# A hybrid decoder layer on one core: 1/rms of x and h sent through DRAM to all partitions and read with a stride, a new head, idle matmuls ahead of the last spread

## The chip, the core and the metric

The kernel runs on one core of a Trainium2 chip. The metric is the device time of one execution in microseconds; the medians below are those of repeated executions. The profile is that of one further execution, taken by the hardware profiler. Engines: PE is TensorE (PEld its loading of weights, beside the matmuls), DVE VectorE, ACT ScalarE, POOL GpSimd, SP SyncE. SP does no arithmetic and issues most of the DMAs.

## The reference, cut to what matters

One layer: an HGRN2 group of four heads and a sliding-window attention group of eight heads, both reading the same normed x; an output projection; a gated MLP with a causal depthwise convolution of three taps; a last norm. x is 1 x 2048 x 1024 in float32, the MLP is 2816 wide.

```python
def rmsnorm(x, w, eps=EPS):
    xf = x.astype(jnp.float32)
    inv = lax.rsqrt(jnp.mean(xf * xf, axis=-1, keepdims=True) + eps)
    return (xf * inv * w.astype(jnp.float32)).astype(x.dtype)
...
        u = rmsnorm(h, norm_mix_w[l])
        proj = u @ w_in[l]
...
        mix = jnp.concatenate([o_hg, o_att], axis=-1)
        h = h + mix @ w_out[l]
        v = rmsnorm(h, norm_ffn_w[l])
        gate = causal_depthwise_conv(v @ w_gate[l], conv_w[l], conv_b[l])
        h = h + (jax.nn.silu(gate) * (v @ w_up[l])) @ w_down[l]
    return rmsnorm(h, final_norm_w)
```

The factor 1/rms belongs to a token. Activations lie with features on the 128 partitions and tokens along the row, so the factor must lie, for all 1024 tokens of a half, on every partition. Since it is the same for all features of a token, it is multiplied in after a projection instead of before.

## The kernel before, in words

**Data.** The 2048 tokens go in two halves of 1024 (`HALF`; `hf` counts them). A tile of activations is 128 features by 1024 tokens; D = 1024 makes 8 of them (`KT`). A matmul takes a 128x128 tile of weights and 512 tokens, so that the two blocks of 512 of a half (`halves()`) fill two PSUM banks. Float32 is made of two parts, hi (rounded) and lo (the rest), by ScalarE (hi) and VectorE (lo): `prep` for weights, `split` for activations. Each product is three matmuls: hi·hi, hi·lo, lo·hi.

**Stages of a half.** A *unit* (L194 to L213) is a projection of 128 columns: 8 tiles of x, 48 matmuls. First come the units k and v of attention (`kv`), then f of the first HGRN head (`f0`), and then heads of HGRN and of attention in turn (hq, g, q units, chunk states, scores). Then the output projection with the residual (h), then gate and up: 22 tiles of 128 of the MLP's width, two at a time (`pr` = 0 to 10, a *pair*), first the gate's pair unit, then the up's. A pair unit (L784) is one Strassen-Winograd step: seven products of four tiles each, named by their weights A11, A12, S2, S1, S3, S4, A22, on the banks X, Y, Z, with sums of the banks' copies (s, u) made by ScalarE (copy, L807) and VectorE (add, L904 and L862 to L866). Then the down projection, with the second half's first units beside it, and the last norm.

**1/rms.** `Stats` (L230 to L276) adds the squares of the tiles (square on ScalarE, sum on VectorE) into one tile `acc` (named invb). `inverse` (L249) sums over the partitions with 8 small matmuls against a column of ones (L258, `pst`, 128 tokens each: token c·128+p comes to partition p, column c), takes 1/sqrt on VectorE in some eleven small steps (L160 to L172, without a table), and multiplies the result with the identity into `acc` (L263): a block per 128 tokens with the factors on its diagonal. `spread` (L267) multiplies that with a 128x128 of ones (L273, `pinv`, two matmuls of 512 columns), which sums each column and so puts it on all partitions, and ScalarE copies it back to `acc` (L276).

This is done for x (named "x"), for h after the output projection ("h") and for the last norm ("o", in quarters of a half). Those who multiply with invb: k and v (L336), q of attention (L358), f (L448), q and g of HGRN (L453, L475), the gate's products (L866) and the product behind Silu (L898). `rs`, the [128, 8] tile itself, is used for v of HGRN.

**Order.** Each engine has its own order of instructions. It is written by the order of calls and a scheduler at build, and pinned in places by `tc.issue_after`. The hooks `then` of a unit or pair unit call something ahead of its i-th tile or of a named product. Ahead: x of the first half is loaded and split, k and v are made from x tile by tile, `constants()` follows (its DMAs on ScalarE's queue), then `xs.inverse`, and `xs.spread` in the middle of unit f. In the second half `inverse` stands behind the last tile but one of unit k and `spread` in the middle of unit v. For h, `inverse` is called ahead of product S4 and `spread` ahead of A22 of the first gate unit; the gate's four products with invb wait until then (`later`, `flush`).

**The end.** The last quarter's `inverse` uses ScalarE's Sqrt, then a spread of 256 columns (L273), eight products (L1105) and the output's DMAs.

Of the kernel before, what the change touches and what calls it, by code (L numbers as in the profile page):

```python
# [8 lines left out]
F32 = mybir.dt.float32  # L9
# [8 lines left out]
P = 128  # L18
# [26 lines left out]
WARM = 12  # L45
LV = 4
# [3 lines left out]
def hymba_layer(ctx: ExitStack, tc: tile.TileContext, a: dict, out: bass.AP):  # L50
# [33 lines left out]
    nc.scalar.activation(warm, ones[:, 0:1], AF.Sigmoid)  # L84
# [5 lines left out]
    idle = ps("at", "idle")  # L90
    for _ in range(WARM):
        nc.tensor.matmul(idle[:, 0:P], ones, ones, start=True, stop=True)
# [12 lines left out]
    def constants():  # L105
# [21 lines left out]
        nc.scalar.dma_start(battn, a["b_attn"])  # L127
# [3 lines left out]
        nc.scalar.dma_start(C.hgw, a["hg_norm_w"])  # L131
        C.sinkb = cp.tile([P, ATT_J, 2], F32, name="sinkb")
        nc.scalar.dma_start(C.sinkb.rearrange("p j k -> p (j k)"), a["sinks"].to_broadcast([P, 8]))
        C.nfw = cp.tile([P, KT], F32, name="nfw")
        nc.scalar.dma_start(C.nfw, a["norm_ffn_w"])
        C.fnw = cp.tile([P, KT], F32, name="fnw")
        nc.scalar.dma_start(C.fnw, a["final_norm_w"])
        C.cw = cp.tile([P, FT, 4], F32, name="cw")
        nc.scalar.dma_start(C.cw, a["conv"])

        lbl = cp.tile([P, 2, HG], F32, name="lbl")
        nc.scalar.dma_start(lbl, a["lb_logits"])
# [38 lines left out]
    def prep(src, slots=False, parts=(slice(0, D),), between=[]):  # L181

        raw = raw4(None)
        hi, lo = [hp.tile([P, D], F32R, tag="m", name=f"w{t}", bufs=KT) if slots else
                  wp.tile([P, D], F32R, tag=t, name=f"w{t}", bufs=2) for t in ("hi", "lo")]
        for c in parts:
            nc.sync.dma_start(raw[:, c], src[:, c])
            nc.scalar.copy(hi[:, c], raw[:, c])  # L188
            nc.vector.tensor_tensor(lo[:, c], raw[:, c], hi[:, c].bitcast(F32), op=ALU.subtract)  # L189
            if between:  # L190
                between.pop(0)()
        return hi, lo

    def unit(src, X, name, order=range(KT), kind="mm", then={}, behind={}, in_turn=False):  # L194
# [5 lines left out]
        for both in [[h] for h in halves()] if in_turn else [halves()]:  # L200
            for i, kt in enumerate(order):
# [6 lines left out]
                with tc.issue_after(mark) if mark else ExitStack():  # L208
                    for w, x, f, l in ((wh, xh, kt == order[0], False), (wh, xl, False, False),
                                       (wl, xh, False, kt == order[-1])):  # L210
                        for b, bs in both:
                            nc.tensor.matmul(o[b], w, x[:, bs], start=f, stop=l)  # L212
# [16 lines left out]

    class Stats:  # L230


        def __init__(self, acc, sq=None, eng=None, k=0):
            self.acc, self.sq, self.eng, self.k = acc, sq, eng or [nc.vector], k

        def halves(self):
            n = self.acc.shape[-1] // 2
            return [Stats(self.acc[:, i * n:(i + 1) * n], self.sq, self.eng, self.k) for i in range(2)]

        def add(self, src, apart=False):  # L240
            t = self.acc if self.k == 0 else self.sq()[:, 0:src.shape[-1]] if self.sq else src
            nc.scalar.activation(t, src, AF.Square)
            self.k += 1
            if self.k > 1 and apart:
                return t
            if self.k > 1:
                return self.eng[(self.k - 1) % len(self.eng)].tensor_tensor(self.acc, self.acc, t, op=ALU.add)

        def inverse(self, keep, last=None):  # L249
# [5 lines left out]
            for src in (self.acc, last):  # L255
                if src is not None:
                    for c in range(nt):
                        nc.tensor.matmul(st[:, c:c + 1], src[:, c * P:(c + 1) * P], ones[:, 0:1],  # L258
                                         start=src is self.acc and (c == 0 or last is None), stop=last is None or src is last,
                                         skip_group_check=last is not None)  # L260
            rs = self.rs = rsqrt(st[:, 0:nt], nt, 1.0 / D, keep, last is not None)
            dg = self.acc
# [4 lines left out]
        def spread(self, bank=None):  # L267
# [3 lines left out]
            for b in range(n // w):  # L271
                pb = ps(aux[b % 2 if bank is None else bank], "pinv")[:, 0:w]
                nc.tensor.matmul(pb, ones, self.acc[:, b * w:(b + 1) * w], start=True, stop=True)  # L273
# [11 lines left out]
    def load(hf, X, stage, W=None):  # L285

        st = Stats(inv_tile())
        xt = []

        def part(kt, c):  # L290
            nc.sync.dma_start(xt[kt][:, c], a["xT"][kt, :, hf * HALF + c.start:hf * HALF + c.stop])
            split(xt[kt][:, c], nmw[:, kt:kt + 1], dst=[t[:, c] for t in X[kt]])

        for kt in range(KT):
# [927 lines left out]
```

## Time and profile before

| what | value |
|---|---|
| median of 3 runs | 2199.68 us (2198.82 to 2201.12) |
| profiled execution | 2200.38 us |
| its span, first to last instruction | 2198.7 us, 29491 instructions |
| mean granted clock of TensorE | 0.997 |
| PE busy | 2177.5 us (99%), 11410 matmuls |
| PEld busy | 1831.0 us (83%) |
| DVE busy | 1639.2 us (75%), 2449 instructions |
| ACT busy | 1049.8 us (48%), 1846 instructions |
| POOL busy | 6.4 us, 28 instructions |
| SP's queue (hardware) | 251.70 MB, 33.9% of 16 engines' span |
| ScalarE's queue | 4.34 MB |

The profiled execution lasted 1.7 us longer than its span; it is 0.7 us above the median of the runs. How rows are read: in a timeline row stand start and duration in us, engine, line, operation, output<-inputs, shape, and a count; where several instructions are drawn together, the duration runs from the first one's start to the last one's end; in square brackets stand the idle time of the engine before it and what ended it. In a row of groups stand, behind the bar, busy time, mean ns of one, and idle time before with its releaser. In a row of waits stand the waiting and the releasing instruction and, behind the colon, us in all, how many times, and the longest. In a row of stretches stand length, the busy time of PE, PEld, DVE, ACT and POOL with instructions, the granted clock, the DMA engines' busy share and GB/s. In a row of DMA issues stand count, size of one and the median time from issue to landing.

### The profile page before, as it was taken

The numbers are of one execution on the slowest core, as the hardware profiler recorded it, in microseconds if no ns is written. First come the engines' busy times: TensorE is split into PE (matmuls) and PEld (weight loads), VectorE is DVE, ScalarE is ACT, GpSimd is POOL, SyncE is SP. The second block draws the span as 40 slices with busy tenths as digits, with TensorE's granted clock in tenths as the row PEclk, the third lists the DMA queues.
The fourth block names the chain that finished last, engine by engine and source line by source line (L and its number), as shares of the span: only waits on it lengthen the run. The fifth ranks groups of instructions, "written<-read, shape, count | busy, mean of one in ns | idle before, by whom it ended". The sixth has DMA issues, their size and how long they took to land.

```text
span 2198.7 us, 29491 instructions
## 1 busy us (share of the span) xinstructions
PE 2177.5 (99%) x11410; PEld 1831.0 (83%) x11410; DVE 1639.2 (75%) x2449; ACT 1049.8 (48%) x1846; POOL 6.4 (0%) x28
## 2 busy tenths in 40 slices
PE   9999999999999999999999999999999999999998
PEld 7988988888888888888889889888888888888887
DVE  6568559688887888885855666677888878887766
ACT  5446445454444444435635455535644444443353
POOL 1000000000000000000000000000000000000000
PEclk9999999999999999999999999999999999999999
DMA  4101112322323234974631111114132323259643
GB/s 154 51 30 51 37 35 76 116 77 92 115 94 122 86 123 139 373 251 138 218 133 41 44 36 51 61 36 134 58 127 90 125 92 114 94 185 395 227 144 130
DMA packets 94214, 257.91 MB, mean 117 GB/s; under 512 B 11578, under 2 KB 17402, under 8 KB 94074
## 3 DMA queue, kind: packets, MB, share of 16 engines
q1 hardware_dynamic: 88128, 251.70, 33.9%
q10 hardware_dynamic: 5946, 4.34, 0.7%
q8 instruction: 89, 1.46, 0.3%
q14 instruction: 51, 0.42, 0.1%
HBM read 195.10 MB, written 57.15 MB: 115 GB/s over the span
## 4 chain that ended last, share of the span: by engine, by line
PE 96%; DVE 2%; ACT 0%; DMA 0%; issue 0%; ACTq 0%; DVEq 0%
PE X L800 7%; PE X L801 7%; PE X L802 7%; PE pop L212 7%; PE hq L212 4%; PE q L212 4%; PE f L212 4%; PE g L212 4%; PE pdx L1011 4%; PE Y L802 4%; PE pdx L1013 4%; PE pdx L1012 4%; PE Y L801 4%; PE Y L800 4%; PE pdy L1011 3%; PE pdy L1013 3%
## 5 line engine op out<-in xcount | busy, mean ns | idle before, releaser
L629 ACT CAST whi<-raw 128x1024 fp32r<-128x1024 f32 x88 | 92.7, 1053 | 109.6 <-PE X L801 67.6
L800 PE MATMUL X<-T,whi 128*128 128x512 f32 x352 | 136.9, 389 | 0.0
L801 PE MATMUL X<-T,whi 128*128 128x512 f32 x352 | 136.9, 389 | 0.0
L802 PE MATMUL X<-T,wlo 128*128 128x512 f32 x352 | 136.9, 389 | 0.0
L895 DVE SCALAR_TENSOR_TENSOR y<-ga,cw,y 128x1024 f32<-128x1024 f32 x88 | 112.3, 1278 | 26.0 <-ACT y L893 25.9
L807 ACT COPY u<-X 128x512 f32<-128x512 f32 x88 | 51.4, 584 | 134.2 <-PE X L802 134.1
L188 ACT CAST whi<-raw 128x1024 fp32r<-128x1024 f32 (+2 forms) x61 | 62.8, 1034 | 96.9 <-PE q L212 31.9
L630 DVE TENSOR_TENSOR wlo<-raw,whi 128x1024 fp32r<-128x1024 f32 x88 | 107.1, 1217 | 0.0
L630 DVE TENSOR_TENSOR xld<-raw,xhd 128x1024 fp32r<-128x1024 f32 x72 | 80.7, 1131 | 19.2 <-ACT xhd L629 18.8
L629 ACT CAST xhd<-raw 128x1024 fp32r<-128x1024 f32 x72 | 69.7, 978 | 41.6 <-DMA raw<-act0T 13.6
L212 PE MATMUL pop<-XL,whi 128*128 128x512 f32 x256 | 85.9, 393 | 2.1 <-DVE XL L224 2.1
L212 PE MATMUL pop<-XH,wlo 128*128 128x512 f32 x256 | 85.0, 391 | 0.8 <-DVE wlo L189 0.8
L212 PE MATMUL pop<-XH,whi 128*128 128x512 f32 x256 | 84.8, 396 | 0.2
L189 DVE TENSOR_TENSOR wlo<-raw,whi 128x1024 fp32r<-128x1024 f32 (+2 forms) x61 | 73.2, 1204 | 10.5 <-ACT whi L188 10.5
L801 PEld LDWEIGHTS X<-T,whi 128*128 128x128 f32 x352 | 66.1, 188 | 13.8
L802 PEld LDWEIGHTS X<-T,wlo 128*128 128x128 f32 x352 | 66.1, 188 | 13.7
L800 PEld LDWEIGHTS X<-T,whi 128*128 128x128 f32 x352 | 66.0, 188 | 13.7
L1011 PE MATMUL pdx<-xhd,hid 128*128 128x512 f32 x192 | 74.5, 392 | 1.0 <-ACT hid L629 1.0
L1012 PE MATMUL pdx<-xld,hid 128*128 128x512 f32 x192 | 74.7, 389 | 0.0
L1013 PE MATMUL pdx<-xhd,lod 128*128 128x512 f32 x192 | 73.7, 389 | 0.0
L621 PE MATMUL pvv<-whi,XH 128*128 128x256 f32 x256 | 73.5, 288 | 0.0
L622 PE MATMUL pvv<-whi,XL 128*128 128x256 f32 x256 | 72.6, 284 | 0.0
(368 smaller groups left out, 6547.0 us busy)
## 6 DMA issues: line engine op xcount, KB each, us to landing
wr<-in_w_down SPq DMA_DIRECT2D x90, 512.0 KB, 4.8
raw<-in_w_gate SPq DMA_DIRECT2D x44, 512.0 KB, 3.6
raw<-in_w_up SPq DMA_DIRECT2D x44, 512.0 KB, 3.7
raw<-act0T SPq DMA_DIRECT2D x20, 512.0 KB, 5.7
raw<-act1T SPq DMA_DIRECT2D x20, 512.0 KB, 10.1
act0B<-y SPq DMA_DIRECT2D x33, 256.0 KB, 2.6
act1B<-y SPq DMA_DIRECT2D x33, 256.0 KB, 2.5
raw<-in_w_out SPq DMA_DIRECT2D x16, 512.0 KB, 4.6
```

Source lines behind the costliest of these rows:

```text
L189: nc.vector.tensor_tensor(lo[:, c], raw[:, c], hi[:, c].bitcast(F32), op=ALU.subtract)
L212: nc.tensor.matmul(o[b], w, x[:, bs], start=f, stop=l)
L621: nc.tensor.matmul(o[:, 0:256], xh[:, t], hi[:, c], start=kt == 0, stop=False)
L629: return (nc.scalar.copy(h, src), (eng or nc.vector).tensor_tensor(l, src, h.bitcast(F32), op=ALU.subtract))
L630: (eng or nc.vector).tensor_tensor(l, src, h.bitcast(F32), op=ALU.subtract))
L800: nc.tensor.matmul(o, wh[:, ws], xh, start=i == 0 and not more, stop=False, skip_group_check=more)
L801: nc.tensor.matmul(o, wh[:, ws], xl, start=False, stop=False, skip_group_check=more)
L802: r = nc.tensor.matmul(o, wl[:, ws], xh, start=False, stop=i == 3, skip_group_check=more)
L895: nc.vector.scalar_tensor_tensor(y, g[:, w:w + HALF], C.cw[:, ft, w:w + 1], y, op0=ALU.mult, op1=ALU.add)
L1011: nc.tensor.matmul(o, wh[:, i, c], ah[:, i, cols], start=f, stop=False, skip_group_check=more)
L1012: nc.tensor.matmul(o, wh[:, i, c], al[:, i, cols], start=False, stop=False, skip_group_check=more)
L1013: nc.tensor.matmul(o, wl[:, i, c], ah[:, i, cols], start=False, stop=l, skip_group_check=more)
```

## The change

1. **x and h.** With `sent=True`, `inverse` ends behind 1/sqrt: GpSimd's queue writes the [128, 8] tile to DRAM as it lies (`row`, 4 KB), and a second DMA of the same queue reads these 1024 numbers to all 128 partitions of `acc` (512 KB). As it lies means partition by partition: the number of token c·128+p stands at p·8+c. So `every()` gives a reader a view with steps of 8 elements (32 bytes) for neighbouring tokens, and the readers' other operands go through `by_tile()`. The product with the identity, the spread's two matmuls and the two copies are gone for x and h of both halves; they stay for the last norm.
2. **The head.** `head()` replaces `load` and `first_unit` for the first half. The first k weights come in three parts over SP's and ScalarE's queues, steps of k and v alternate, squares of x come where `turn` puts them, the constants' DMAs move from ScalarE's queue to SP's, behind x, and their arithmetic behind the last sum. The first HGRN head waits in order for that sum. The load of the Sigmoid table stands behind ScalarE's first fetches.
3. **The end.** Seven 128x128 matmuls in float32 on a bank that nobody reads (`TAIL_WARM`) follow `pst` of the last quarter.

The diff, cut to its core:

```diff
+TAIL_WARM = 7
...
-        nc.scalar.dma_start(battn, a["b_attn"])
+        nc.sync.dma_start(battn, a["b_attn"])
...
+    def every(invb, bs=slice(0, HALF)):
+        return invb.rearrange("q (t c) -> q c t", c=TT)[:, bs.start // P:bs.stop // P]
+
+    def by_tile(t):
+        return t.rearrange("p (c t) -> p c t", t=P)
...
+            if last is not None:
+                without_use(ps("at", "idle"), TAIL_WARM, marks["pst"])
             rs = self.rs = rsqrt(st[:, 0:nt], nt, 1.0 / D, keep, last is not None)
+            if sent:
+                row = dp.tile([P, nt], F32, name=f"row{len(sent_rows)}")
+                sent_rows.append(row)
+                nc.gpsimd.dma_start(row, rs)
+                nc.gpsimd.dma_start(self.acc, row.rearrange("p c -> (p c)").unsqueeze(0).to_broadcast([P, n]))
+                return
             dg = self.acc
...
+    def head(X):
...
+        k0, k1, k2 = slice(0, P), slice(P, 4 * P), slice(4 * P, D)
+        v0, v1 = slice(0, 2 * P), slice(2 * P, D)
+        nc.sync.dma_start(raw[0][:, k0], a["w_att"][ATT_J][:, k0])
+        for c in (k1, k2):
+            fetched = nc.scalar.dma_start(raw[0][:, c], a["w_att"][ATT_J][:, c])
+        with tc.issue_after(fetched.ins):
+            nc.scalar.activation(warm, ones[:, 0:1], AF.Sigmoid)
+        for kt in range(KT):
+            for c in [h for _, h in halves()] if kt == 0 else [slice(0, HALF)]:
+                nc.sync.dma_start(xt[kt][:, c], a["xT"][kt, :, c])
+            if kt == 1:
+                nc.sync.dma_start(raw[1], a["w_att"][ATT_J + 1])
+        nc.sync.dma_start(raw[2], a["w_f"][0])
...
+        turn(cut, *W[0], raw[0], k0)
+        tile_of_x(0)
+        step(0, 0)
+        turn(cut, *W[0], raw[0], k1)
+        tile_of_x(1)
+        step(0, 1)
+        turn(cut, *W[0], raw[0], k2)
+        turn(cut, *W[1], raw[1], v0)
+        for kt in range(2):
+            step(1, kt)
+        for kt in range(2, KT):
+            tile_of_x(kt)
+            if kt == 2:
+                turn(cut, *W[1], raw[1], v1)
             else:
+                turn(st.square, xt[kt - 3])
+            for u in range(2):
+                step(u, kt)
...
+        with tc.issue_after(on_act[-1].ins), tc.issue_after(summed.ins):
+            constants()
+        with tc.issue_after(on_pe[-1].ins):
+            st.inverse("x", sent=True)
+        with tc.issue_after(marks["pst"].ins):
+            f0 = unit(F, X, "f", kind="aux")
+        return o, st.acc, st.rs, f0, summed
...
-                nc.vector.tensor_tensor(dst[:, bs], o[b], invb[:, bs], op=ALU.mult)
+                nc.vector.tensor_tensor(by_tile(dst[:, bs]), by_tile(o[b]), every(invb, bs), op=ALU.mult)
...
-                iv = invb[:, j * 512:(j + 1) * 512]
+                iv = every(invb, slice(j * 512, (j + 1) * 512))
...
-                later.append(lambda: nc.vector.tensor_tensor(dst, x, iv, op=ALU.mult))
+                later.append(lambda: nc.vector.tensor_tensor(by_tile(dst), by_tile(x), iv, op=ALU.mult))
...
-            then = {"S4": lambda: hs.inverse("h"), "A22": lambda: (hs.spread(), flush())} if pr == 0 else {}
+            then = {"S4": lambda: hs.inverse("h", sent=True), "A22": flush} if pr == 0 else {}
...
-                nc.vector.tensor_tensor(y, y, invb, op=ALU.mult)
+                nc.vector.tensor_tensor(by_tile(y), by_tile(y), every(invb), op=ALU.mult)
...
-        kv = [first_unit(X, None, 0, {3: lambda: s1.inverse("o"), 7: lambda: xs.inverse("x")})]
-        kv.append(first_unit(X, None, 1, {2: lambda: (s1.spread(), finish(hf, hh, s1, lo, [nc.sync])), 4: xs.spread}))
+        kv = [first_unit(X, 0, {3: lambda: s1.inverse("o"), 7: lambda: xs.inverse("x", sent=True)})]
+        kv.append(first_unit(X, 1, {2: lambda: (s1.spread(), finish(hf, hh, s1, lo, [nc.sync]))}))
```

The change's longer text shifts the line numbers: the product of k and v with invb is L429 there (L336 before), that of f L542 (L448), the gate's L961 (L866), the matmuls of a pair unit L895 to L897 (L800 to L802), ScalarE's bank copy L902 (L807), the hi cast L724 (L629).

What this does to the orders of the engines is shown at three places. First VectorE at x of the first half: the end of the 1/sqrt (y), and the first readers. Before:

```order
L170 TENSOR_TENSOR t<-y 128x8
L171 TENSOR_TENSOR t<-t,ms 128x8
L172 SCALAR_TENSOR_TENSOR y<-t,y 128x8
L263 TENSOR_TENSOR invb<-ident,y 128x1024
L336 TENSOR_TENSOR kT<-kv_192,invb 128x512
L336 TENSOR_TENSOR vT<-kv_242,invb 128x512
L336 TENSOR_TENSOR kT<-kv_193,invb 128x512
L336 TENSOR_TENSOR vT<-kv_243,invb 128x512
L448 TENSOR_TENSOR f<-f_378,invb 128x512
```

Of the change, first the beginning of the same chain (ms and y; lbm, lb and omlb are constants of HGRN):

```order
L164 TENSOR_SCALAR ms<-pst 128x8
L153 RECIPROCAL lbm<-lbm 128x4
L170 TENSOR_SCALAR y<-ms 128x8
L155 TENSOR_TENSOR lb<-lbe,lbm 128x4
L174 TENSOR_TENSOR t<-y 128x8
L157 TENSOR_SCALAR omlb<-lb 128x4
```

Three operations of constants stand between its steps there. Then its end and the readers:

```order
L176 SCALAR_TENSOR_TENSOR y<-t,y 128x8
L429 TENSOR_TENSOR kT<-kv_140,invb 128x512
L429 TENSOR_TENSOR kT<-kv_141,invb 128x512
L429 TENSOR_TENSOR vT<-kv_142,invb 128x512
L429 TENSOR_TENSOR vT<-kv_143,invb 128x512
L542 TENSOR_TENSOR f<-f_385,invb 128x512
```

The product with the identity is gone, and both blocks of k now stand ahead of those of v. On POOL there are four pairs of DMAs, two for x and two for h; the first two of these rows are x of the first half:

```order
L286 DMA row_382<-y 128x8
L287 DMA invb<-row_382 128x1024
L286 DMA row_4378<-y 128x8
L287 DMA invb<-row_4378 128x1024
L286 DMA row_9172<-y 128x8
L287 DMA invb<-row_9172 128x1024
L286 DMA row_13256<-y 128x8
L287 DMA invb<-row_13256 128x1024
```

On POOL's queue these are the only DMAs; ahead of them stand the constants' masks. Second, VectorE at h of the first half (ga is the gate's result with its halo; S, raw and wlo belong to the weights of the next pair). Before:

```order
L172 SCALAR_TENSOR_TENSOR y<-t,y 128x8
L263 TENSOR_TENSOR invb<-ident,y 128x1024
L866 TENSOR_TENSOR ga<-ga,invb 128x512 x4
L759 TENSOR_TENSOR S<-raw 128x512
L904 TENSOR_TENSOR s_4483<-Z,s_4483 128x512
```

Of the change:

```order
L176 SCALAR_TENSOR_TENSOR y<-t,y 128x8
L999 TENSOR_TENSOR s_4480<-Z,s_4480 128x512
L725 TENSOR_TENSOR wlo<-raw,whi 128x1024
L961 TENSOR_TENSOR ga<-ga,invb 128x512 x4
L854 TENSOR_TENSOR S<-raw 128x512
L990 SCALAR_TENSOR_TENSOR y<-ga,cw,y 128x1024
L855 TENSOR_TENSOR S<-S,raw 128x512
```

The first sum of the up unit and a wlo of its weights stand ahead of the products with invb now, and one S behind them. ScalarE at the same place, before:

```order
L807 COPY s_4483<-X 128x512
L807 COPY u_4512<-X 128x512
L276 COPY invb<-pinv 128x512 x2
L891 COPY halo<-ga 128x2
L893 ACTIVATE y<-ga,cw 128x1024
```

Of the change:

```order
L902 COPY s_4480<-X 128x512
L724 CAST whi<-raw 128x1024
L902 COPY u_4509<-X 128x512
L902 COPY s_4524<-Y 128x512
L986 COPY halo<-ga 128x2
L988 ACTIVATE y<-ga,cw 128x1024
```

The copies of invb are gone, and the copies of two products of the up unit stand ahead of halo and y, which wait for the gate's products. Third, TensorE at the start of that up unit (X, Y, Z are its banks; whi and wlo A11's or A12's weights, Sh and Sl those of the sums). Before:

```order
L800 MATMUL X<-B_3755,whi 128x512
L801 MATMUL X<-B_3756,whi 128x512
L802 MATMUL X<-B_3755,wlo 128x512
L800 MATMUL X<-T_4169,Sh 128x512
L801 MATMUL X<-T_4170,Sh 128x512
L802 MATMUL X<-T_4169,Sl 128x512
```

Of the change:

```order
L895 MATMUL X<-B_3756,whi 128x512
L896 MATMUL X<-B_3757,whi 128x512
L897 MATMUL X<-B_3756,wlo 128x512
L897 MATMUL Z<-B_3908,wlo 128x512
L895 MATMUL Z<-B_3908,whi 128x512
L896 MATMUL Z<-B_3909,whi 128x512
L897 MATMUL Z<-B_3908,wlo 128x512
L895 MATMUL Z<-B_4094,whi 128x512
```

Before, the next product on X (S2, with Sh) follows the first one directly; now the rest of Z and twelve matmuls on Y stand between them.

More of the change, by code (lines that the diff above doesn't have):

```diff
@@ L88, in hymba_layer, with without_use @@
                             base=0, pattern=[[-1, P]], channel_multiplier=1)
-    idle = ps("at", "idle")
-    for _ in range(WARM):
-        nc.tensor.matmul(idle[:, 0:P], ones, ones, start=True, stop=True)
+    def without_use(bank, n, behind=None):
+        with tc.issue_after(behind.ins) if behind else ExitStack():
+            for _ in range(n):
+                nc.tensor.matmul(bank[:, 0:P], ones, ones, start=True, stop=True)
+    without_use(ps("at", "idle"), WARM)
     state = cp.tile([P, HG, P], F32, name="state")
@@ L319, in rows, with first_unit @@
+    def first_unit(X, i, then={}):
+        return unit(a["w_att"][ATT_J + i], X, "kv", then=then)
     def rows(kv):
@@ L1106, in finish @@
             queues[d % len(queues)].dma_start(out[d, :, hf * HALF + bs.start:hf * HALF + bs.stop], t)
-    X, W = [], []
-    for xs in load(0, X, lambda: slot("x"), W):
-        pass
-    kv = [first_unit(X, W, i) for i in range(2)]
-    constants()
-    xs.inverse("x")
-    f0 = unit(a["w_f"][0], X, "f", kind="aux", then={4: xs.spread})
-    nxt = X, kv, xs.acc, xs.rs, f0
+    X = []
+    *nxt, summed = X, *head(X)
     for hf in range(NH):
```

140 lines of the change are left out of this document (82 added, 58 removed).

## The prediction

> **What bounds the kernel now.** The page comes first: its span, the busy times and the chain of work that ended last.
>
> ```profile
> span 2198.7 us, 29491 instructions
> PE 2177.5 (99%) x11410; PEld 1831.0 (83%) x11410; DVE 1639.2 (75%) x2449; ACT 1049.8 (48%) x1846; POOL 6.4 (0%) x28
> PE 96%; DVE 2%; ACT 0%; DMA 0%; issue 0%; ACTq 0%; DVEq 0%
> ```
>
> TensorE is busy for 99% and carries 96% of the chain, so an edit is worth the TensorE time that it removes, and costs something only where it makes TensorE stop. In all TensorE stands for 21.2 us (2198.7 - 2177.5). Next come the waits of TensorE, in all, times, longest:
>
> ```profile
> PE pop L212 <- DVE XL L224: 2.1, 2, 1.4
> PE pinv L273 <- DVE invb L263: 1.9, 1, 1.9
> PE kv L212 <- ACT XH L226: 1.7, 1, 1.7
> PE X L800 <- ACT s L807: 1.5, 2, 0.7
> ```
>
> They are short and single. Then the busy time by stretch (PE, PEld, DVE, ACT, POOL): one of the mixer, one of gate/up.
>
> ```profile
> 200.00:400.00 200.00, 197.56 (x1384) 170.88 (x1383) 134.29 (x268) 95.14 (x254) 0.00 (x0) 1.00 0.15 45
> 680.00:720.00 40.00, 40.00 (x178) 33.11 (x177) 32.75 (x43) 17.84 (x26) 0.00 (x0) 1.00 0.28 99
> ```
>
> VectorE is idle for a third of the mixer, but for only 7.25 of 40 us in gate/up; that is the cover for everything that the change gives to VectorE.
>
> **The spreads that go.** The timeline of TensorE around the spread of h, in the first half:
>
> ```profile
> 461.62 0.39 PE L800 MATMUL X<-B,whi 128*128 128x512 f32 x1
> 464.34 0.39 PE L800 MATMUL Z<-B,whi 128*128 128x512 f32 x1
> 482.51 0.39 PE L800 MATMUL X<-B,whi 128*128 128x512 f32 x1
> 485.00 0.39 PE L802 MATMUL X<-B,wlo 128*128 128x512 f32 x1
> 486.12 0.50 PE L800 MATMUL X<-T,Sh 128*128 128x512 f32 x1 [0.73 <-ACT s L807]
> 488.77 0.39 PE L802 MATMUL X<-T,Sl 128*128 128x512 f32 x1
> 489.00 1.88 PE L273 MATMUL pinv<-invb,ones 128*128 128x512 f32 x4
> 490.95 0.40 PE L801 MATMUL Z<-B,whi 128*128 128x512 f32 x1
> ```
>
> Twelve matmuls of product A11 take 464.34 - 461.62 = 2.72 us, 0.227 each from start to start. Without the spread the second Z matmul would start at 489.00 + 0.23 = 489.23; it starts at 490.95. A spread of 1024 columns thus costs TensorE 1.7 us. Two such (h in both halves) and that of x for the second half stand inside work without waits: **-1.7 x 3 = -5.1 us**. The eight copies by ScalarE and the four products with the identity by VectorE that go with them were off TensorE's path.
>
> In the same place the order of the change moves ten Z and twelve Y matmuls between the up unit's first product and its S2. S2 accumulates on the bank that ScalarE first copies out: its start at 486.12 instead of 485.23 is a stop of 0.9 us, once in each half (the 1.5 us x2 above are its named part). With 22 matmuls between, 5.0 us against a copy of 0.6, it is covered: **-1.8 us**. Nothing else is late there: Z's operands are A11's weights and tiles that the same unit has read already.
>
> **What replaces them: two DMAs through DRAM on POOL's queue.** They do not occur in the trace, so they are bounded by its DMA rows, issue to landing:
>
> ```profile
> raw<-in_w_g SPq DMA_DIRECT2D x8, 512.0 KB, 4.7
> raw<-in_w_q SPq DMA_DIRECT2D x8, 512.0 KB, 3.5
> raw<-act1T SPq DMA_DIRECT2D x20, 512.0 KB, 10.1
> keep<-h SPq DMA_DIRECT2D x32, 256.0 KB, 2.3
> odd<-moved ACTq DMA_DIRECT2D x6, 1.0 KB, 1.9
> ```
>
> The write is 4 KB, the read 512 KB. Low end: 1.9 + 3.5 = 5.4 us; high end, with the slowest class of 512 KB loads: 1.9 + 10.1 = 12.0. The write goes to DRAM as keep does, and the DMA engines are as lightly used here as for w_g: I take 2.3 + 4.7 = **7.0 us**. What POOL itself adds is shown nowhere, which is why I don't take the low end. [...]
>
> In the **second half's x**, two whole units lie between the sum and the first reader, so the trip is covered. In the **first half's x** it is not. The rows of VectorE and TensorE there:
>
> ```profile
> 36.65 0.16 DVE L160 TENSOR_SCALAR ms<-pst 128x8 f32<-128x8 f32 x1
> 38.66 0.17 DVE L172 SCALAR_TENSOR_TENSOR y<-t,y 128x8 f32<-128x8 f32 x1
> 46.81 0.69 DVE L336 TENSOR_TENSOR kT<-kv,invb 128x512 f32<-128x512 f32 x1 [6.66 <-ACT invb L276]
> 48.94 0.39 PE L212 MATMUL hq<-XH,whi 128*128 128x512 f32 x1
> ```
>
> 1/rms is ready at 38.8; the change puts three small constants' operations into the chain (0.2 each), so 39.4, and kT can start at 46.4. All four mm banks hold k and v, so hq waits for the first kT product: 0.69 + 0.47 (below), hence 47.7 against 48.94. Unit f without its spread would end at 48.94 - 1.7 = 47.2. So **-1.2 us** (bounds: -1.7 at a trip below 6.5, +3.8 at 12).
>
> In the **h** place VectorE stands until invb lands:
>
> ```profile
> 486.49 0.17 DVE L172 SCALAR_TENSOR_TENSOR y<-t,y 128x8 f32<-128x8 f32 x1
> 490.67 2.50 DVE L866 TENSOR_TENSOR ga<-ga,invb 128x512 f32<-128x512 f32 x4 [2.75 <-ACT invb L276]
> ```
>
> 1/rms is ready at 486.7, invb at 493.7 instead of 490.7. Behind the four products on VectorE stand S, y and S of the next weights; behind halo, y and Sh on ScalarE stands the copy u<-X of the up unit, which TensorE needs before A22. From landing to that copy's end: 4 x 1.07 + 0.6 + 1.2 + 0.7 + 1.05 + 0.6 = 8.4 us. A22 is 98 matmuls behind the up unit's first in the new order: 482.51 + 98 x 0.227 = 504.8. So TensorE stops only if invb lands after 496.4, a trip over 9.7 us: **0** (bound: 2.3 a half at 12).
>
> **The strided read.** In the new layout neighbouring tokens of invb lie 32 bytes apart. The nearest rows are the decay products L539, whose two inputs and output have steps of 8, 16 and 32 bytes at 512, 256 and 128 elements, against unbroken operations of 256 and 128:
>
> ```profile
> L539 DVE TENSOR_TENSOR f<-f 128x512 f32<-128x512 f32 x8 | 5.7, 717 | 0.0
> L539 DVE TENSOR_TENSOR f<-f 128x256 f32<-128x256 f32 x8 | 5.2, 656 | 0.1
> L539 DVE TENSOR_TENSOR f<-f 128x128 f32<-128x128 f32 x8 | 3.3, 408 | 0.0
> L247 DVE TENSOR_TENSOR invb<-invb,fsq 128x256 f32<-128x256 f32 x7 | 3.0, 423 | 1.6 <-ACT fsq L242 1.6
> 3.16 0.29 DVE L189 TENSOR_TENSOR wlo<-raw,whi 128x128 fp32r<-128x128 f32 x1 [1.23 <-ACT whi L188]
> ```
>
> (656 - 423)/256 and (408 - 290)/128 both give 0.9 ns an element. One stream of three is strided now: between 0 and 0.9; I take 0.92 in full, since no row shows a single stream. That is 0.47 us for 512 elements and 0.94 for 1024. A pair of gate/up tiles has four L866 and two L898: 3.8 us more per pair (38 us), against 7.25 idle in 40. The cover halves and holds. In the mixer 56 such operations take 26 us more of VectorE, a third idle; some start a chain that TensorE waits for, so I charge **+1.0 us** for all (0 to 5).
>
> [...]
>
> **The head.** The new order puts constants' DMAs behind x and interleaves k and v. Granted clock (after POOL's column):
>
> ```profile
> 10.00:11.00 1.00, 0.00 (x0) 0.00 (x0) 0.00 (x0) 1.00 (x2) 0.00 (x0) 0.58 1.08 422
> 16.00:17.00 1.00, 1.00 (x4) 0.73 (x3) 1.00 (x3) 1.00 (x2) 0.00 (x0) 0.50 0.95 377
> 17.00:18.00 1.00, 1.00 (x6) 0.83 (x5) 1.00 (x2) 0.98 (x2) 0.00 (x0) 1.00 1.02 418
> 9.93 1.15 ACT L226 ACTIVATE XH<-x,nmw 128x1024 fp32r<-128x1024 f32 x1 [1.50 <-DMA sinkb<-in_sinks]
> ```
>
> TensorE waits for x's second tile (ScalarE 9.93, DMA engines full), then runs without a stop, at half clock until 17.2. The tile has as many bytes ahead of it as before (64 + 448 + 512 KB), less some constants: **-0.5 us**. If the clock returns half of that stage earlier, -1.7; later, +1.7.
>
> **The tail.** Seven idle matmuls (14 records) run while VectorE makes the last 1/rms:
>
> ```profile
> 71.64 1.95 PE L467 MATMUL pdiag<-hg,K 128*128 128x128 f32 x16
> 2191.25 1.21 PE L273 MATMUL pinv<-invb,ones 128*128 128x256 f32 x2 [1.85 <-DVE invb L263]
> ```
>
> At full clock 14 x 0.122 = 1.7 us; pst ends at 2189.4, so they are done by 2191.1, ahead of the spread. It took 1.21 us at half clock; at full 0.6. I take **-0.3** (-0.6 to +1.4).
>
> **The sum** against the profiled execution's 2200.38: -5.1 - 1.8 - 1.2 + 0 + 1.0 - 0.5 - 0.3 = -7.9, 2192.5. The median of the runs lies 0.7 below that execution: **2191.8 us**.
>
> **Rivals.** (1) *VectorE stops TensorE in gate/up.* In 679 to 694 VectorE has no gap; one L866 and two L898 there add 2.3 us of lag. If the bank copies and weights behind it have less slack, each of the 44 units stops TensorE by, say, 0.3 us: +13, 2205. It becomes the bound outright at 7.25 us more a pair, 1.8 ns an element, twice the rows'. Against it: TensorE waited for nothing in that window. Slower; 0.09. (2) *The trip is long.* From 9.7 us on each microsecond costs three (x once, h twice); the gain is gone near 12, and at 14 it is 2206. For it: POOL's share is unseen. Slower; 0.07. (3) *Only the spreads count*: the stop before S2 moves to another copy, x gains nothing: -5.1 + 1.0 = -4.1, 2195.6, within 0.2%. For it: freed waits often pass to the next in order. 0.2. (4) *The clock returns early* in the head: 2190.1. 0.1. The forecast has 0.54.
>
> **Range and chances.** About 0.2% (4.4 us) is what a measurement of this kernel can tell from no change. Faster below 2195.3: 0.54 + 0.1 and little of (3): 0.65; same 0.21; slower 0.14. The range runs from the forecast with its low bounds (x -0.5, clock -1.7, strides -1.0, tail -0.3: 2188.3) past (3) to the edge of (1) and (2): 2188 to 2199.
>
> **What would show it.** No pinv for x and h; three TensorE stretches 1.7 us shorter; X L800 no longer waiting for s; hq's first matmul 1.2 to 1.7 us earlier against pst; L866's and L898's successors at about 1150 and 2150 ns. Wrong it would be if new waits of TensorE on ScalarE's u copies or VectorE's wlo appear in gate/up, if invb lands over 9.7 us after 1/rms, or if strided operations cost nothing and the mixer's +1.0 falls away.

## The result, and the profile after

The change takes 2206.8 us (median of 7 runs, 2205.3 to 2209.5) against 2199.7 (7 runs, 2197.8 to 2204.0): a ratio of 1.0036, 95% interval 1.0026 to 1.0046. Slower by 0.36%, where 2191.8 was forecast. Its page:

```profile
span 2205.1 us, 29446 instructions
PE 2177.5 (99%) x11408; PEld 1831.0 (83%) x11408; DVE 1740.3 (79%) x2447; ACT 1048.1 (48%) x1840; POOL 10.5 (0%) x36
PE 86%; DVE 10%; issue 2%; DMA 2%; ACT 1%; SPq 0%; DVEq 0%; POOLq 0%; ACTq 0%
```

VectorE has 101 us more, ScalarE nothing, and the chain that ended last goes through VectorE for 10% of the span instead of 2%. TensorE's waits, longest first:

```profile
PE pdx L1106 <- ACT hid L724: 4.3, 2, 2.1
PE pop L212 <- DVE XL L224: 3.6, 3, 2.2
PE Y L895 <- ACT Sh L724: 2.4, 2, 1.2
PE pdx L1106 <- DVE y L1001: 1.8, 2, 1.1
PE X L895 <- ACT whi L724: 1.4, 2, 0.7
```

13.5 us, where the kernel before had 2.1 on XL, 1.0 on hid and 1.5 on s. The stretches below run from the start of one matmul to the start of another: gate/up from its first to its last matmul (the first products of down stand among its last ones), the rest of down from there to down's last matmul, and the last row from there to the end of the span. They are given for the kernel before, the change, and two kernels of the experiments: e14 is the change with 1/rms read without the stride, e16 a version that sorts the tokens with a small matmul.

| from, to | before | change | e14 | e16 |
|---|---|---|---|---|
| start to first k matmul | 6.25 | 6.41 | 6.48 | 6.64 |
| k of the first half to f of the second head | 110.94 | 105.97 | 107.29 | 106.06 |
| rest of mixer and out projection, to gate/up | 344.43 | 346.77 | 344.44 | 344.42 |
| gate/up, first half | 426.94 | 427.11 | 424.13 | 424.67 |
| rest of down, first half | 207.76 | 212.99 | 209.06 | 208.09 |
| second half, to gate/up | 452.87 | 453.66 | 451.37 | 452.00 |
| gate/up, second half | 426.94 | 427.44 | 424.13 | 424.67 |
| rest of down, second half | 211.41 | 214.14 | 212.45 | 211.88 |
| end | 11.11 | 10.57 | 10.57 | 10.55 |

The head won 5 us; every later stretch but the end is longer than before. Where and how, in three places. **The end of the mixer**, VectorE and TensorE in the second half of the change:

```profile
1436.84 1.10 DVE L570 TENSOR_TENSOR hg<-g,invb 128x512 f32<-128x512 f32 x1
1439.91 1.06 DVE L570 TENSOR_TENSOR hg<-g,invb 128x512 f32<-128x512 f32 x1
1440.88 1.22 DVE L224 TENSOR_TENSOR XL<-hg,XH 128x1024 fp32r<-128x1024 f32 x1
1442.16 0.73 PE L212 MATMUL pop<-XL,whi 128*128 128x512 f32 x2 [2.19 <-DVE XL L224]
```

Two products with the stride are among VectorE's last operations ahead of XL, for which TensorE waits. Before, the same row was:

```profile
1440.03 0.73 PE L212 MATMUL pop<-XL,whi 128*128 128x512 f32 x2 [1.38 <-DVE XL L224]
```

The wait grew from 1.38 to 2.19 us, 0.8 more for two times 0.4. **The first pairs of gate/up**, where VectorE had stood for invb, in stretches of 40 us (columns as in the prediction; the first two rows are of the kernel before):

```profile
500.00:540.00 40.00, 40.00 (x178) 33.10 (x178) 34.89 (x46) 18.86 (x27) 0.00 (x0) 1.00 0.32 105
540.00:580.00 40.00, 40.00 (x178) 33.14 (x177) 34.04 (x44) 18.18 (x26) 0.00 (x0) 1.00 0.30 98
```

The same two of the change, and one that TensorE passes without a stop:

```profile
500.00:540.00 40.00, 39.16 (x172) 31.78 (x171) 40.00 (x45) 20.11 (x29) 0.00 (x0) 1.00 0.29 99
540.00:580.00 40.00, 40.00 (x178) 33.07 (x177) 38.48 (x45) 17.47 (x27) 0.00 (x0) 1.00 0.33 106
680.00:720.00 40.00, 40.00 (x178) 33.15 (x177) 36.78 (x43) 18.71 (x28) 0.00 (x0) 1.00 0.30 99
```

VectorE is full in the first and nearly full in the second, and its backlog reaches TensorE. At 530 us TensorE waits 0.7 us for whi, a cast of weights that stands in ScalarE's order behind halo and y, which wait for VectorE's products with invb; at 590 us it waits 1.1 us for Sh, the cast of a sum of weights that VectorE makes. **The start of down**, ScalarE, TensorE and VectorE:

```profile
881.63 2.14 DVE L993 TENSOR_TENSOR y<-y,invb 128x1024 f32<-128x1024 f32 x1
887.63 0.62 ACT L724 CAST xhd<-raw 128x512 fp32r<-128x512 f32 x1 [0.90 <-DMA raw<-act0B]
888.15 1.04 ACT L724 CAST hid<-wr 128x1024 fp32r<-128x1024 f32 x1
889.25 0.50 PE L1106 MATMUL pdx<-xhd,hid 128*128 128x512 f32 x1 [2.15 <-ACT hid L724]
891.98 0.80 PE L1106 MATMUL pdx<-xhd,hid 128*128 128x512 f32 x1 [0.72 <-DVE y L1001]
```

hid, which TensorE needs next, stands behind xhd in ScalarE's order, and xhd waits for a DMA of what VectorE's late products made. Before, hid stood ahead of that xhd:

```profile
888.82 1.05 ACT L629 CAST hid<-wr 128x1024 fp32r<-128x1024 f32 x1 [1.64 <-PE X L801]
890.61 0.62 ACT L629 CAST xhd<-raw 128x512 fp32r<-128x512 f32 x1 [0.74 <-DMA raw<-act0B]
```

And some time is lost twice, since there are three stretches at half clock (column behind POOL's):

```profile
368.00:372.00 4.00, 4.00 (x33) 3.27 (x32) 2.87 (x7) 0.59 (x1) 0.00 (x0) 0.57 0.00 0
890.00:897.00 7.00, 6.28 (x16) 4.45 (x16) 7.00 (x10) 3.14 (x3) 0.00 (x0) 0.53 0.98 359
1443.00:1447.00 4.00, 4.00 (x16) 3.39 (x15) 4.00 (x9) 0.28 (x1) 0.00 (x0) 0.57 0.88 251
```

4 x 0.43/0.5 is 3.4 us at half clock, then 6.6 and 3.4: 6.7 us lost. The profile of the kernel before had none between its head and its end. The second and third stretch begin 1.1 and 1.2 us behind the ends of the stops of 2.15 and 2.19 us shown above. The first, 1.7 us of the loss, is not shown to come of the stride: in the 3.4 us ahead of it TensorE waited only 0.69 us, as the kernel before does at that place; and e3 and e8, with x's stride, have none there (granted clock 1.00 from 368 to 372 us).

### The profile page after: what moved, and what is told of

Read it like the earlier page. It is cut to its first block, busy times and chain, and to the rows that moved or that the text cites. A ratio compares the mean times of both kernels' runs of the same rounds, so it can differ in the third digit from the quotient of the medians.

```text
span 2205.1 us, 29446 instructions
## 1 busy us (share of the span) xinstructions
PE 2177.5 (99%) x11408; PEld 1831.0 (83%) x11408; DVE 1740.3 (79%) x2447; ACT 1048.1 (48%) x1840; POOL 10.5 (0%) x36
## 4 chain that ended last, share of the span: by engine, by line
PE 86%; DVE 10%; issue 2%; DMA 2%; ACT 1%; SPq 0%; DVEq 0%; POOLq 0%; ACTq 0%
PE pop L212 7%; PE X L897 5%; PE X L895 5%; PE X L896 5%; PE hq L212 4%; PE q L212 4%; PE g L212 4%; PE f L212 4%; PE pdx L1108 4%; PE pdx L1106 4%; PE pdx L1107 3%; PE Y L895 3%; PE Y L896 3%; PE Y L897 3%; PE pdy L1108 3%; PE pdy L1107 3%
## 5 line engine op out<-in xcount | busy, mean ns | idle before, releaser
L895 PE MATMUL X<-T,whi 128*128 128x512 f32 x352 | 137.3, 390 | 0.0
L897 PE MATMUL X<-T,wlo 128*128 128x512 f32 x352 | 137.0, 389 | 0.0
L724 ACT CAST whi<-raw 128x1024 fp32r<-128x1024 f32 x88 | 92.2, 1050 | 75.5 <-PE X L896 44.9
L190 ACT CAST whi<-raw 128x1024 fp32r<-128x1024 f32 x57 | 59.6, 1050 | 91.8 <-PE q L212 32.2
L993 DVE TENSOR_TENSOR y<-y,invb 128x1024 f32<-128x1024 f32 x44 | 94.4, 2146 | 0.0
L961 DVE TENSOR_TENSOR ga<-ga,invb 128x512 f32<-128x512 f32 x68 | 77.4, 1146 | 9.7 <-DMA invb<-row 8.4
L724 ACT CAST Sh<-S 128x1024 fp32r<-128x1024 f32 (+1 forms) x46 | 46.7, 1016 | 76.2 <-DVE S L855 76.2
L724 ACT CAST xhd<-raw 128x1024 fp32r<-128x1024 f32 x72 | 69.3, 977 | 25.6 <-DMA raw<-act1T 5.5
L902 ACT COPY u<-X 128x512 f32<-128x512 f32 x88 | 51.3, 583 | 57.1 <-PE X L897 57.0
L895 PEld LDWEIGHTS X<-T,whi 128*128 128x128 f32 x352 | 66.1, 188 | 14.8 <-ACT u L902 1.2
L897 PEld LDWEIGHTS X<-T,wlo 128*128 128x128 f32 x352 | 66.1, 188 | 13.9
```

Of the source, the lines that this page charges most:

```text
L724: return (nc.scalar.copy(h, src), (eng or nc.vector).tensor_tensor(l, src, h.bitcast(F32), op=ALU.subtract))
L895: nc.tensor.matmul(o, wh[:, ws], xh, start=i == 0 and not more, stop=False, skip_group_check=more)
L897: r = nc.tensor.matmul(o, wl[:, ws], xh, start=False, stop=i == 3, skip_group_check=more)
L961: later.append(lambda: nc.vector.tensor_tensor(by_tile(dst), by_tile(x), iv, op=ALU.mult))
L993: nc.vector.tensor_tensor(by_tile(y), by_tile(y), every(invb), op=ALU.mult)
```

## The experiments

All medians are of runs beside runs of the kernel before on the same chip (its median 2199.8 to 2200.9); ratios are to that. The change itself ran beside the kernel before only for the result above, so differences between its median and an experiment's carry some 1 us between the batches.

**e1, e2, e3: sums over partitions taken with a step**, so that the row lies in the order of tokens (e1 both, e2 x, e3 h).

```diff
-  matmul(st[:, c:c + 1], src[:, c * P:(c + 1) * P], ones[:, 0:1])
+  matmul(st[:, c:c + 1], src.rearrange("p (t c) -> p c t", c=nt)[:, c], ones[:, 0:1])
+  # for x: rs for v of HGRN, a new [128, 8] tile
+  nc.gpsimd.dma_start(self.rs, row.rearrange("p c -> (p c)").rearrange("(c t) -> t c", t=P))
```

> 1/rms of x and h still goes through DRAM on POOL's queue, in the same order on TensorE and VectorE, but its token sums are taken from the accumulated squares with a step (token p*8+c comes to partition p, column c), so that the row in DRAM lies in the order of tokens and invb is read without a stride. A second small DMA per half brings the [128, 8] tile that v of HGRN needs. Stride theory: the change lost its gain because VectorE's strided reads reach TensorE at eight places (350, 530, 590, 889, 1442, 1624, 1684, 1983 us) and the stops let the clock fall three times; without the stride VectorE is busy for about 1640 us again, the stops go (10.6 us) and so do the 13.7 us at half clock (6.8 us): about 2189.5 us (2187 to 2192). Rival, order theory: the stops come from the new order and the trip through DRAM, the strides are covered: 2205 to 2208 us.

> Only x's 1/rms lies in the order of tokens; h's is still read with a stride. Stride theory: the two waits of the output projection for XL fall back to what they were before the change (by 1.2 us in all) and the clock's falls at 368 and 1443 us are gone (3.4 us); the stops in gate/up and at the start of down stay, with the fall at 890: about 2202 us (2200 to 2204). Order theory: 2205 to 2208 us.

> Only h's 1/rms lies in the order of tokens; x's is still read with a stride. Stride theory: the four stops in gate/up (3.8 us), those at the two starts of down (5.6 us more than before) and the clock's fall at 890 us (3.4 us) are gone, the waits of the output projection stay with their two falls of the clock: about 2194 us (2192 to 2197). Order theory: 2205 to 2208 us.

Measured: e1 2217.7 us (1.0082, 1.0068 to 1.0096), e2 2219.6 (1.0095, 1.0082 to 1.0109), e3 2202.9 (1.0012, 1.0003 to 1.0021). Neither theory had that. VectorE was back at 1635.7 us in e1, but TensorE's busy time rose by 20 us: gate/up took 433 us in e1, without a stop, and 432 in e2. Both have the new tile; e3 has none and took 427.6 and 426.0. And the stepped sums are slow themselves; in e3:

```profile
470.76 3.74 PE L281 MATMUL pst<-ones,invb 128*128 128x1 f32 x16
```

These took 1.84 us without a step, and a half-clock stretch followed here in e1 and e3. So e1 to e3 changed more than the stride and decide little.

**e5: the old head.** The change with `load`, `first_unit` and the constants of the kernel before.

> The change with the head of the kernel before (load, first units and constants as they were), the rest kept. Head theory: the new head itself brings some 3.5 us of the 4.8 us by which hq now starts earlier, and x's trip through DRAM the rest: 2210 us (2209 to 2212). Rival: the 4.8 us come from the spread of x that is gone and from kT's earlier start, with either head: 2207 us (2206 to 2208).

2206.7 us (1.0038, 1.0025 to 1.005), the same as the change; f of the second head came at 114.3 us (before 117.2, change 112.4). The time speaks for the rival.

**e8: 64 bytes of tiles that nobody reads.**

```diff
+  nc.vector.memset(sp.tile([P, TT], F32, tag="pad", name="pad"), 0.0)
```

> The change and one [128, 8] tile of 32 bytes in two buffers that nobody reads, in the pool of small tiles: it moves the tiles of gate/up's and down's operands (T, B, S) by 64 bytes in SBUF and nothing else. Address theory: in e1 and e2 matmuls of gate/up followed each other at 0.229 us instead of 0.2267 because of this shift, not because of the layout of 1/rms: 10 to 13 us slower than the change, 2218 us. Rival (the extra DMA or the stepped sums did it): 2206 us.

2217.6 us (1.008, 1.0066 to 1.0094), gate/up 432.0 and 432.5 us: the address theory holds against its rival, since e8 has neither the extra DMA nor the stepped sums. One stretch of e8, to be compared with that of the change above:

```profile
680.00:720.00 40.00, 40.00 (x176) 32.63 (x175) 36.61 (x42) 18.20 (x27) 0.00 (x0) 1.00 0.30 99
```

176 matmuls in 40 us instead of 178, at full clock and without a stop.

**e9, e10, e11: the write to DRAM sorts; a pin at down.**

```diff
-  nc.gpsimd.dma_start(row, rs)
+  nc.gpsimd.dma_start(row.rearrange("c t -> t c"), rs)        # e9, e10: 4-byte pieces, no stride for readers
...
+  with tc.issue_after(marks["hid"].ins) if k == 5 and t is raw else ExitStack():   # e10, e11
       made = split_into(h, l, t, nc.vector)
+  if k == 1:
+      marks["hid"] = made[0]
```

> The write to DRAM puts the 1024 numbers of x and of h in the order of tokens (4-byte pieces), the read to all partitions and everything else is as in the change, the order of the engines too; invb is read without a stride, the sums over partitions have no step and no tile is added. Stride theory: the stops in gate/up (3.8 us) and the longer waits of the output projection (1.2 us) go, part of those at the starts of down (3 us), and most half-clock stretches that came with them (3 to 7 us): 2194 us (2191 to 2198), VectorE busy for about 1640 us. Order theory: 2204 to 2208 us.

> As e9, and at the start of down the cast of the second piece of weights (hid) is pinned ahead of the cast of the sixth piece of activations (xhd of 512), as it stood before the change. Theory of two causes: what e9 leaves at the two starts of down (some 1.2 and 1.9 us, with a half-clock stretch) is this order: 2 to 5 us less than e9, about 2190 us. Stride theory alone: the same as e9 within 1 us.

> The change with that pin alone, strides kept. Theory of two causes: VectorE, behind by its strided products, and the order each hold the first products of down; with the pin a part of the 2.9 and 3.2 us goes: 2203 us (2201 to 2205). If the strides alone hold it: 2206 us within 1.

e9 2215.5 us (1.0075, 1.0063 to 1.0088), e10 2212.9 (1.0055, 1.0041 to 1.0069), e11 2205.6 (1.0022, 1.0013 to 1.0031). The sorting write made the trip long; POOL's DMAs and the stop that came of it in e9, in h of the first half:

```profile
492.43 0.90 POOL L286 DMA_DIRECT2D row<-y  x1 [445.85 <-DVE y L176]
502.62 0.56 POOL L287 DMA_DIRECT2D invb<-row  x1 [9.29 <-DMA row<-y]
...
513.57 0.50 PE L895 MATMUL Y<-T,Sh 128*128 128x512 f32 x1 [3.66 <-ACT Sh L724]
```

1/rms was ready at 492.1 and invb landed at 507.5: 15.4 us, and 3.7 us of stop. This is the prediction's rival (2), a long trip, and it covered what e9 and e10 were to show: neither came near its forecast. Away from those stops e10 is close to the kernel before: 344.43 us from f to gate/up, 207.69 in the first down (before 344.43 and 207.76), 212.02 in the second (before 211.41). e11 has the median that the strides alone would give, but a ratio that is 3 us below the change's, with intervals that overlap: its time decides nothing. In its profile the pin moves the wait: at the first start of down the first stop falls from 2.15 to 0.78 us and the next grows from 0.72 to 1.82.

**e14, e15: the stride alone.** Orders, DMAs and addresses are those of the change; in the trace of e14 the instructions of every engine come in the change's order.

```diff
-  return invb.rearrange("q (t c) -> q c t", c=TT)[:, bs.start // P:bs.stop // P]
+  return invb[:, bs]
...
-  return t.rearrange("p (c t) -> p c t", t=P)
+  return t
```

> The change in everything (orders, trip, DMAs, addresses), but invb is read without a stride although the row lies partition by partition, so that most tokens are multiplied with the 1/rms of another token: only the time of the strided reads is taken out. Stride theory: the output projection's longer waits (1.2 us) and the half-clock stretches at 368 and 1443 us (3.4 us) go, the four stops in gate/up (3.8 us) and some 3 us at the starts of down: 2195.5 us (2193 to 2198). Rival (the strides are covered but for the output projection): 2203 to 2206 us.

> As e14 (the same tokens' mix), with the pin of e10 at the starts of down. Theory of two causes: e10 had the waits of the kernel before at all places but those of its long trip; without that trip the forecast's sum is left, 2190 to 2194 us. If something else in the change costs time (the new head's half-clock stretches, the trip), it stays above 2196 us.

e14 2191.6 us (0.9963, 0.9951 to 0.9976), e15 2189.6 (0.9955, 0.9942 to 0.9969). Both are a little below their forecast ranges. Without the stride the change is 15.2 us faster than with it (16 by the ratios), and faster than the kernel before. TensorE's waits in e14:

```profile
PE pdx L1106 <- ACT hid L724: 3.1, 2, 1.6
PE pop L212 <- DVE XL L224: 2.1, 2, 1.4
```

The waits for Sh, whi and y are gone, that for XL is what it was before, and no stretch at half clock is left between head and end. In e15, with the pin, hid is back at the 1.0 us of before:

```profile
PE pdx L1109 <- ACT hid L724: 1.0, 2, 0.5
```

**e17, e18: the stride of x's readers alone, of h's alone.** The same edit for one of them.

> As e14, for x alone: the readers of x's 1/rms (k, v, q, f, hq, g) take it without a stride, so most tokens get another token's factor; h's readers keep the stride. If the 15 us of e14 are made where the profile of the change is longer than that of e14, x's share is what its two mixers are longer, 2.3 us each with their half-clock stretches: 2202 us (2200 to 2204). Rival: the strides in the mixer have VectorE's idle third as cover and cost nothing: 2206.8 us within 1.

> As e14, for h alone: the readers of h's 1/rms (the gate's products and the product behind Silu) take it without a stride, x's readers keep it. By the same sections h's share is 3.0 and 3.3 us in gate/up and 3.9 and 1.7 us in down: 2195 us (2193 to 2197). Rival: gate/up covers its strides and the time is in the mixer: 2204 us or more.

e17 2204.2 us (1.0016, 1.0007 to 1.0025), e18 2194.9 (0.9979, 0.997 to 0.9988): x's strides cost 2.7 us, h's 11.9, together 14.6 of the 15.2. By the ratios it is 4.4 and 12.5 of 16.1, so x's share is known only to a microsecond or two. Both rivals are out.

**e19: e14 with the old head.**

> As e14 (both read without a stride), with the head of the kernel before. If the new head brings what the profiles show beside the clock (f of the second head 113.8 us in e14, 114.3 us in e5), it is 0.5 us slower than e14: 2192 us. If the head is worth the 3.4 us of two half-clock stretches that the profile of the kernel before had and that of the change had not: 2195 us.

2193.8 us (0.9969, 0.9956 to 0.9981), between the two forecasts; the intervals of e14 and e19 overlap. The new head is worth 0 to 2 us by e5 and e19.

**e12, e16: the order of tokens by a small matmul** that turns the tile; each token has its own factor.

```diff
-  nc.gpsimd.dma_start(row, rs)
+  turned, at = st[0:nt, P:2 * P], self.acc[0:nt, 0:P]
+  nc.tensor.matmul(turned, rs, ident, start=True, stop=True)
+  nc.scalar.copy(at, turned)
+  nc.gpsimd.dma_start(row, at)                                  # row is [8, 128] now
```

> A version with the reference's values and no stride: the [128, 8] tile is turned to [8, 128] by one small matmul with the identity, copied by ScalarE and written to DRAM as 8 rows of 512 bytes, so that it lies there in the order of tokens; three tiles of unit f lie between the sums and this matmul, and product S4 in the gate's unit. Two causes: neither strides nor the order at down are left (its order at the start of down is already that of the pin): 2192 to 2196 us, e15 plus about 1.5 us for a longer way to invb and hq's later start. Rival: the turn makes the trip longer than 9.7 us, and the stops of e9 come back in part: 2200 us or more.

> As e12 (the reference's values, no stride), with the small matmul that turns the tile pinned as early as 1/rms is there: behind two tiles of unit f for x of the first half, ahead of products S1 and S2 of the first up unit for h; and with the pin of e10 at the starts of down. It should have e15's time and what the turn costs: four small matmuls of 0.35 us and up to 1 us of waiting in the head: 2191.5 us (2190 to 2194), faster than both kernels. Rival: the longer way to invb still stops TensorE in the first up unit or at hq, with half-clock stretches: 2196 us or more.

e12 2198.9 us (0.9997, 0.9988 to 1.0006): its turn came late, at 39.4 us in the head where 1/rms was ready at 35.7, and hq stopped for 2.9 us, behind which its matmuls ran at half clock (0.43 us from start to start instead of 0.23): between its forecast and its rival. e16, with the turn pinned early, 2193.7 us (0.9968, 0.9957 to 0.998): faster than both kernels. Its page:

```profile
span 2189.0 us, 29472 instructions
PE 2171.5 (99%) x11416; PEld 1827.6 (83%) x11416; DVE 1633.0 (75%) x2447; ACT 1047.8 (48%) x1844; POOL 10.5 (0%) x36
```

**e6: no idle matmuls at the end.** `TAIL_WARM = 0`.

> The change without the seven idle matmuls behind the last sums. If they keep the clock up for the last spread, the end (from the last matmul of down to the end of the span) is 0.5 us longer than the 10.6 us of the change, as it was before (11.1 us); else it stays 10.6 us.

In its one run the end was 11.09 us, as before the change; in the change it is 10.57.

## Why the prediction was wrong

The step that failed is one term of the sum: "so I charge +1.0 us for all (0 to 5)" for the strided read. It measured 15.2 us (e14 against the change). Without this term the sum gives 2190.8 us, and e14 took 2191.6. That they lie so near is in part luck: e14's two downs are 2.3 us longer than before, which the sum did not have, and its head (k to f of the second head) is 3.65 us shorter where 1.7 was forecast, with 1.7 of it a half-clock stretch less. The other terms, point by point:

- **The spreads and the stop before S2**, -1.7 x 3 and -1.8. In e14 each gate/up is 2.81 us shorter than before (2.6 forecast), and the second half up to gate/up 1.50 (1.7). Right; in the change the stops that the strides make eat it up.
- **The trip**, 7.0 us, harmless for h up to 9.7. Right within 1 us; the low end of 5.4 us was too short. Issues of the change for h, and VectorE's first reader:

```profile
484.48 0.55 POOL L286 DMA_DIRECT2D row<-y  x1 [445.52 <-DVE y L176]
488.03 0.55 POOL L287 DMA_DIRECT2D invb<-row  x1 [3.00 <-DMA row<-y]
492.17 4.32 DVE L961 TENSOR_TENSOR ga<-ga,invb 128x512 f32<-128x512 f32 x4 [4.36 <-DMA invb<-row]
```

1/rms was ready at 484.2 and invb landed at 492.1, so 8.0 us, and 6.9 for x; no stop followed in e14, and at 15.4 us (e9) one did.
- **x of the first half**, -1.2: from pst to hq 12.79 us instead of 14.49, -1.7. **The head**, -0.5: -3.6 in the profile, 3.4 of which is that its two half-clock periods did not come in this execution (e14 had one); by e5 and e19 0 to 2 us. **The end**, -0.3: -0.5 (e6).
- **The strided read's price** for one operation, 0.47 and 0.94 us, was right. The groups of the change:

```profile
L993 DVE TENSOR_TENSOR y<-y,invb 128x1024 f32<-128x1024 f32 x44 | 94.4, 2146 | 0.0
L961 DVE TENSOR_TENSOR ga<-ga,invb 128x512 f32<-128x512 f32 x68 | 77.4, 1146 | 9.7 <-DMA invb<-row 8.4
```

In e14 the same groups have means of 1219 and 690 ns: 0.93 and 0.46 us more with the stride of 32 bytes, 0.9 ns an element, as in the L539 rows of the kernel before: here a single strided stream of three cost what three cost there.

What failed was the step from that price to TensorE. I read the cover of VectorE from one steady stretch (680 to 720 us, 7.25 us idle of 40) and held it for all of gate/up. There it did hold: no stop in that stretch, in the change either. But the cover is thin elsewhere, and rows that I could have read say so: in 500 to 540 us VectorE was busy for 34.89 of 40 already, and the change adds 3.8 and, ahead of it, a wait for invb of 4.36 us (2.75 before); at the last pair, from 870 to 889 us, VectorE was busy for 18.70 of 19, and what it makes late there is what the xhd ahead of hid waits for; at the end of the mixer two of the products that got the stride stand shortly ahead of XL. At those places are the stops that are shorter or gone in e14, and h's readers have 11.9 of the 14.6 us, x's 2.7. The mixer, which I charged, was the smaller part. The sign that I had named, new waits of TensorE in gate/up on u copies or wlo, came as waits on whi and Sh.

My rival (1) named the mechanism, VectorE stopping TensorE, and 2205 us, but as a loss of 0.3 us in each of 44 units; it came as four stops in gate/up and two at each start of down, with the clock falling behind some. That its 2205 lies near the 2206.8 is luck: gate/up is 6.3 us longer than in e14, not 13. I gave it 0.09. The half clock appears in no term of mine outside head and end: of the 15.1 us by which the change's span is longer than e14's, about 8 are the named waits (13.5 against 5.2), 5 the half-clock stretches (13.4 us against 3.4 in e14's head, at half; the one at 368 us and e14's cancel), and the rest is in small stops that I did not add up. The clock's part is not of this execution alone: the mean granted clock was 0.995 to 0.997 in all seven runs of the change and 0.998 in all five of e14.

A second cost that I did not see is the order at the start of down: hid behind xhd. It is most of the 1.3 and 1.0 us by which e14's downs are longer than before; with the pin (e15) 0.3 and 0.5 are left. I compared orders at x, h and S2 only. By medians e15 is not clearly faster than e14.

e16 closes the sum: with each token's own factor, and strides and that order taken out, 2193.7 us is reached, 1.9 over the forecast, with four more small matmuls on TensorE.

## What to carry to other kernels

When an edit hands work to an engine that is not the bound, read that engine's idle time in the fullest stretches (the first after a wait, the last before a stage ends, and right ahead of what the bound engine waits for), not in a typical one. A layout that saves a few instructions of the writer but makes every reader step is paid at each read, here 204 times; sort once, where it is small (4 KB, on TensorE in e16), and not in the DMA (from 1/rms to invb 15.4 us in e9, 8.0 in the change). Take a suspected cost out with all else unchanged before any redesign: e14 decided in one run what e1 to e3 and e9 could not.

## What the runs showed of the hardware

- **64 unread bytes in a pool**, by which the operands of gate/up should lie elsewhere in SBUF (the traces show no addresses), made TensorE's matmuls follow each other at 0.229 instead of 0.2267 us (176 and 178 of them in the rows from 680 to 720 us) and cost some 11 us (e8 against the change). Which operand's address matters, and why, was not tried.
- **The clock can fall after short stops.** The wait for XL of 2.19 us at the end of the second mixer was followed by 3.4 us at half clock in the change and in e3; one of 1.4 us there (before, e14 to e16) was not, and neither was the wait for hid of 2.12 us at the second start of down in the change (granted clock 1.00 from 1984 to 1996 us). At 368 us in the change the clock fell with only 0.69 us of waiting in the 3.4 us before. What decides was not tried.
- **A write that sorts.** The 4 KB write took 9.7 us from issue to landing in e9 (median of four), where neighbouring numbers go to places 512 bytes apart, and 3.0 as it lies in the change. In what pieces it was written the trace does not show: POOL's queue has 704 packets in both kernels.
- **Stepped weights.** Sums over partitions whose weights are loaded with a step of 32 bytes took 3.74 us for 16 matmuls instead of 1.84 (e3); the mean of all 80 loads of this kind, those without the step among them, rose from 192 to 248 ns.
